# Two ConvFFNs, by both halves of the positions at once or by one half after the other, with the converted weights kept in DRAM

## The chip, the cores and the metric

The kernel runs on one core of one Trainium2 chip. The metric is the time of the program on the device in microseconds; the time of a kernel is the median of its runs. Beside the plain runs there is one execution under the hardware profiler, from which the page and the trace come. All numbers of single instructions are from that execution.

## What is computed

Two layers of a decoder trunk over 1024 positions of 1024 channels (batch 1, float32). Layer 0 is a hybrid mixer (attention and a state-space model), layer 1 a Conformer convolution module. Each is followed by a ConvFFN, and the change is about these two:

```python
def conv_ffn(h, up_w, conv_w, conv_b, down_w):
    u = causal_dwconv(h @ up_w.astype(h.dtype), conv_w, conv_b)     # width 3
    gate, val = u[..., :FFN_DIM], u[..., FFN_DIM:]                  # FFN_DIM = 2816
    return (jax.nn.silu(gate) * val) @ down_w.astype(h.dtype)

def conformer_conv(h, pw1_w, pw1_b, dw_w, dw_b, ln_w, ln_b, pw2_w, pw2_b):
    u = h @ pw1_w.astype(h.dtype) + pw1_b.astype(h.dtype)
    u = u[..., :CONF_WIDTH] * jax.nn.sigmoid(u[..., CONF_WIDTH:])
    u = causal_dwconv(u, dw_w, dw_b)                                # width 31
    u = jax.nn.silu(layer_norm(u, ln_w, ln_b))
    return u @ pw2_w.astype(h.dtype) + pw2_b.astype(h.dtype)

for i in range(DEPTH):
    ...
    x = x + conv_ffn(rms_norm(x, ffn_norm_w[i]), ffn_up_w[i], ffn_conv_w[i], ffn_conv_b[i], ffn_down_w[i])
```

## The kernel before, in words

The activations lie with channels on the 128 partitions and positions along the row: eight tiles of 1024 positions, handled as two halves of 512 (h = 0 and 1). The mixer takes the first part of the span and is not touched. What follows is `trunk_tail`: the FFN of layer 0, the Conformer, the FFN of layer 1.

**A product in two 16-bit parts.** `gemm` (line 234) multiplies float32 values as pairs of 16-bit parts: three matmuls (high x high, high x low, low x high) for each of the 8 tiles of the contraction, so 24 matmuls of 128x128 by 512 positions for one tile of one half. The weights' parts are made on the chip by `loads` (line 86): SP's queue loads a raw float32 tile (512 KB) into one of three `raw` buffers; ScalarE scales it into the high part (line 94 or 98); the low part comes either from VectorE in one step (line 99, `pool=False`) or from a second ScalarE step that scales raw in place (line 95) and a subtraction on GpSimd (line 96, `pool=True`). Both parts lie in one of four `w` buffers. The scale is a power of two found from the sum of squares of the whole matrix. These sums come from `scan` (line 138), which loads every weight once more through ScalarE's queue (line 150, two buffers in the trunk) and squares it there (line 147); `rooted`, `powers` and `conf_powers` turn the sums into scales, with small matmuls on TensorE (`total`, line 110) in between.

**The FFN by pairs and groups.** An FFN has 22 pairs (a gate tile and a value tile of 128 columns). `pair` (line 966) multiplies both up tiles, evicts them through the width-3 convolution (`conv3`, lines 946 to 954: one ScalarE step and two VectorE multiply-adds out of PSUM), applies SiLU (line 982) and the product (line 962, on GpSimd where the group is `pool=True`) and squares the result for a scale (line 963). A `Group` is some pairs for one or both halves. `close` turns a group's results into 16-bit parts (lines 936, 937) and `down` multiplies them by the group's rows of the down projection, eight output tiles, adding each to x (line 1065).

**How the work was cut.** Six pairs (BOTH) are done for both halves with one conversion of each weight; the other 16 pairs, as two groups of 8 (HALVES), for half 0 and later again for half 1, with a conversion each time. In layer 0 the order is: the six pairs for both halves, then the groups of half 0, then those of half 1 laid beside the Conformer of half 0. In layer 1: the groups of half 0 laid beside the Conformer of half 1, then the six pairs for both halves, then the groups of half 1. `first_pairs` (line 989) is the start of a both-halves group: two pairs whose four weight tiles are held, first for half 0, while the norm of half 1 (`rms`, line 910) is made after the first two tiles, then for half 1.

**The Conformer** goes half by half too: `p1` (line 1106) has 16 tiles of matmuls and, for each of eight channel tiles, 30 multiply-adds of 512 positions on VectorE (line 1125); `ln` (line 1137) is the LayerNorm, whose sums over the channels go through small matmuls (`token_sums`, line 904, and `bcast`, line 259); `p2` multiplies by the second weights. All Conformer weights are converted with `pool=True`, once for each half.

**What sets the order.** The functions are generators that yield an estimate of TensorE's time (5.2 for an up tile). `along(a, na, b, nb)` takes from b in the ratio nb/na while a goes on, `weave` puts a fixed gap of one generator between the steps of others, `beside` takes one step of the scans per yield, and `ahead` runs a generator for a given cost. What comes out is an order of priorities; loads are raised by AHEAD = 60 instructions and evictions by EV = 100, and a scheduler lays out each engine's instructions at build time. On the chip every engine and every queue then works in that order.

Of the kernel before, what the change touches and what calls it, by code (L numbers as in the profile page):

```python
# [14 lines left out]
F16 = mybir.dt.float16  # L15
# [13 lines left out]
BOTH = 6  # L29
HALVES = (8, 8)  # L30
# [15 lines left out]
class Net:  # L46
    def __init__(self, ctx, tc, I, out):
        self.tc, self.nc, self.I, self.out = tc, tc.nc, I, out
        self.sb = ctx.enter_context(tc.tile_pool(name="sb", bufs=1))
        self.n = 0  # L50
        self.pows, self.sums = {}, {}
# [34 lines left out]
    def loads(self, src, nk, scale, pool=False):  # L86

        nc = self.nc
        with self.tc.high_priority(offset=AHEAD):
# [7 lines left out]
            else:  # L97
# [4 lines left out]
                                               ALU.mult, ALU.subtract)  # L102
        return w
# [862 lines left out]
    def pair(self, G, i):  # L966
# [4 lines left out]
        for e, j2 in enumerate((G.k0 + i, NP + G.k0 + i)):  # L971
            w = self.loads(self.I["ffn_up_w"][G.l, j2], KT, self.pows[f"up{G.l}"][0], pool=G.pool)
            prev = None
            for h in G.hs:
# [12 lines left out]
                yield 5.2  # L987

    def first_pairs(self, G):

        r1 = self.rms(1, self.fnw[:, G.l, :])
        self.open(G)
        js = (G.k0, NP + G.k0, G.k0 + 1, NP + G.k0 + 1)
        G.have = 2
        ws = [self.loads(self.I["ffn_up_w"][G.l, k], KT, self.pows[f"up{G.l}"][0]) for k in js]
        keep = self.T("hf", [P, 2, 22, 2])
        for h in range(2):
            for i, j2 in enumerate(js):
                ps = self.PT("mm")
                self.gemm(ps[:], ws[i], self.hn[h])  # L1000
                with self.tc.high_priority(offset=EV):
                    a = self.conv3(G.l, j2, ps, keep[:, 0, i] if h else None)
                    if j2 < NP:
                        self.nc.scalar.activation(a[:], a[:], AF.Silu)
                        g = a
                    else:
                        self.gate(G, i // 2, h, g, a)
                    if h == 0:
                        self.nc.vector.tensor_copy(keep[:, 0, i], ps[:, HALF - 2:HALF])
                if h == 0 and i < 2:  # L1010
                    steps(r1, 1)
                yield 5.2
# [44 lines left out]
    def down(self, G, post=None):  # L1057
        for c in range(KT):
            w = self.loads(self.I["ffn_down_w"][G.l, c, :, G.k0:G.k0 + G.n, :], G.n,
                           self.pows[f"down{G.l}"][0], pool=G.pool)  # L1060
# [22 lines left out]
    def p1_tile(self, j, h):  # L1083
# [3 lines left out]
        wb = self.loads(self.I["conf_pw1_w"][KT + j], KT, sc, pool=True)  # L1087
# [5 lines left out]
        wa = self.loads(self.I["conf_pw1_w"][j], KT, sc, pool=True)  # L1093
# [74 lines left out]
    def p2(self, h):  # L1168
# [4 lines left out]
        for c in range(KT):  # L1173
            w = self.loads(self.I["conf_pw2_w"][c], KT, self.pows["pw2"][0], pool=True)
# [14 lines left out]
    def halves(self, l, k0):  # L1189

        nb, nh = HALVES
        halo = self.T("hf", [P, 2, 22, 2])
        hb, hc = halo[:, :, 0:nb], halo[:, :, nb:nb + nh]
        return ([Group(l, k0, nb, (h,), hb, pool=h != l) for h in range(2)],
                [Group(l, k0 + nb, nh, (h,), hc, pool=h != l) for h in range(2)])

    def trunk_tail(self):

        self.V, self.s = {}, {}
        A = Group(0, 0, BOTH, (0, 1))  # L1200
        B, C = self.halves(0, BOTH)
# [11 lines left out]
        f = chain(f, self.beside(chain(self.ups(C[1], (B[1], None)), self.call(self.powers, 1),  # L1213
# [191 lines left out]
```

## Time and profile before

| What | us |
|---|---|
| runs, median of 3 | 2300.31 (2294.36 to 2307.05) |
| the profiled execution | 2295.18 |
| its span, first to last instruction | 2293.4 |
| PE busy in the span | 2209.9 |
| mean granted TensorE clock | 0.982 |

The first 600 us or so are the mixer. The first matmul of layer 0's FFN starts at 604 us, the last of layer 1's ends just before 2289.5 us. In a row of a group, the number after x is the count, then come the busy time, the mean duration in ns, and after the bar the idle time of the engine just before these instructions, with what ended it. In a row of a stretch each engine has its busy time and its count, then come the clock that was granted to TensorE, the mean busy share of the 16 DMA engines, and GB/s.

### The profile page before, as it was taken

Reading aid. Unit: us, or ns where it says so; the run is one execution under the profiler, and the core shown is the slowest. Engines: PE = TensorE matmul, PEld = TensorE weight load, DVE = VectorE, ACT = ScalarE, POOL = GpSimd, SP = SyncE. Lnnn points to the kernel's source line nnn. Section 1 sums busy time; section 2 is a strip of 40 time slices with the busy share of each in tenths; the row PEclk is TensorE's granted clock in tenths of the full one; section 3 lists DMA queues with packets and bytes.
Section 4 is the critical chain, followed back from the end, with each engine's and each line's share of the span. In section 5 each row is a group of like instructions: output and inputs, shape, how many; then the busy total and the mean of one; then the engine's idle time right before and its main releaser. Section 6 shows DMA issues by size and latency. Waiting matters only on the chain. (4 is left out here: it accounts for less than half of the span.)

```text
span 2293.4 us, 28980 instructions
## 1 busy us (share of the span) xinstructions
PE 2209.9 (96%) x10767; PEld 1228.2 (54%) x10767; DVE 1549.3 (68%) x2923; ACT 1376.2 (60%) x2191; POOL 452.2 (20%) x336
## 2 busy tenths in 40 slices
PE   7999999889899999999999998999999999999999
PEld 7788987767544444444444444444444444444444
DVE  6976677776755547454789997699997164635763
ACT  7776556653566667576677756677877443514541
POOL 0000000123000000023545543445553400000000
PEclk9999999999899999999999999999999999999999
DMA  6434211221356576755223332333332321133332
GB/s 204 138 98 147 83 28 31 85 71 56 109 185 195 185 245 198 266 172 183 91 82 105 104 97 70 96 92 101 101 102 73 111 65 55 49 113 97 101 102 82
DMA packets 87885, 262.08 MB, mean 114 GB/s; under 512 B 12864, under 2 KB 15552, under 8 KB 87744
## 3 DMA queue, kind: packets, MB, share of 16 engines
q1 hardware_dynamic: 58368, 178.44, 25.1%
q10 hardware_dynamic: 29376, 81.80, 11.2%
q8 instruction: 84, 1.38, 0.2%
q14 instruction: 57, 0.47, 0.1%
HBM read 256.01 MB, written 4.19 MB: 113 GB/s over the span
## 5 line engine op out<-in xcount | busy, mean ns | idle before, releaser
L239 PEld LDWEIGHTS <-w 128*128 128x128 f16 x7488 | 737.2, 99 | 899.8 <-issue 31.1
L239 PE MATMUL pmm<-h,w 128*128 128x512 f16 x5376 | 1173.9, 381 | 10.9 <-DVE h L934 5.0
L239 PE MATMUL pmm<-g,w 128*128 128x512 f16 x2112 | 468.9, 384 | 0.0
L96 POOL TENSOR_TENSOR w<-raw,w 128x1024 f16<-128x1024 f32 x144 | 308.5, 2144 | 492.4 <-ACT raw L95 309.1
L952 DVE SCALAR_TENSOR_TENSOR a<-pmm,c_ffn_conv_w,a 128x511 f32<-128x511 f32 (+1 forms) x352 | 262.0, 746 | 174.3 <-ACT a L946 171.2
L1125 DVE SCALAR_TENSOR_TENSOR pt<-u,c_conf_dw_w,pt 128x512 f32<-128x512 f32 x480 | 339.7, 750 | 8.9 <-ACT pt L1122 5.4
L239 PE MATMUL pmm<-h,whl 128*128 128x512 f32 x912 | 231.8, 404 | 0.0
L147 ACT ACTIVATE scan<-scan 128x1024 f32<-128x1024 f32 (+2 forms) x204 | 173.1, 850 | 71.1 <-DMA scan<-ffn_up_w 45.0
L1065 DVE SCALAR_TENSOR_TENSOR x<-pmm,gs,x 128x512 f32<-128x512 f32 x96 | 71.9, 749 | 174.1 <-PE pmm L239 174.0
L239 PEld LDWEIGHTS pmm<-h,whl 128*128 128x128 f32 x912 | 167.7, 190 | 36.3 <-POOL whl L220 0.2
L429 PE MATMUL pmm<-whl,h 128*128 128x384 f32 (+1 forms) x672 | 137.7, 354 | 18.2 <-ACT h L230 11.5
L963 ACT ACTIVATE a<-g 128x512 f32<-128x512 f32 x88 | 55.3, 628 | 164.3 <-DVE g L962 83.7
L946 ACT ACTIVATE a<-pmm,c_ffn_conv_b,c_ffn_conv_w 128x512 f32<-128x512 f32 x112 | 86.4, 771 | 76.4 <-PE pmm L239 74.3
L429 PEld LDWEIGHTS pmm<-whl,h 128*128 128x128 f32 x672 | 119.3, 193 | 22.5 <-ACT h L230 11.8
L98 ACT ACTIVATE w<-raw,c_su_up 128x1024 f16<-128x1024 f32 x88 | 100.0, 1138 | 48.9 <-PE pmm L239 31.8
L99 DVE SCALAR_TENSOR_TENSOR w<-raw,c_su_up,w 128x1024 f16<-128x1024 f32 x88 | 112.6, 1280 | 18.2 <-ACT w L98 16.8
L98 ACT ACTIVATE w<-raw,c_su_down 128x1024 f16<-128x1024 f32 (+1 forms) x48 | 51.2, 1071 | 70.8 <-PE pmm L239 66.9
L982 ACT ACTIVATE a<-a 128x512 f32<-128x512 f32 x80 | 50.1, 627 | 52.9 <-DVE a L952 42.3
L94 ACT ACTIVATE w<-raw,c_su_pw 128x1024 f16<-128x1024 f32 x48 | 54.7, 1140 | 37.2 <-PE pmm L239 33.6
L94 ACT ACTIVATE w<-raw,c_su_up 128x1024 f16<-128x1024 f32 x64 | 72.6, 1138 | 6.8 <-PE pmm L239 6.8
L95 ACT ACTIVATE raw<-raw,c_su_up 128x1024 f32<-128x1024 f32 x64 | 73.2, 1146 | 2.1
L1032 POOL TENSOR_TENSOR hf<-hf,c_ffn_conv_w 128x8 f32<-128x8 f32 x8 | 4.5, 559 | 341.9 <-DVE hf L980 283.6
(316 smaller groups left out, 2333.6 us busy)
## 6 DMA issues: line engine op xcount, KB each, us to landing
raw<-ffn_up_w SPq DMA_DIRECT2D x152, 512.0 KB, 3.6
raw<-ffn_down_w SPq DMA_DIRECT2D x64, 512.0 KB, 3.5
raw<-conf_pw_w SPq DMA_DIRECT2D x48, 512.0 KB, 3.6
scan<-ffn_up_w ACTq DMA_DIRECT2D x88, 256.0 KB, 3.1
scan<-ffn_up_w ACTq DMA_DIRECT2D x44, 512.0 KB, 4.6
scan<-ffn_down_w ACTq DMA_DIRECT2D x32, 512.0 KB, 4.1
scan<-conf_pw_w ACTq DMA_DIRECT2D x24, 512.0 KB, 4.3
raw<-w_out SPq DMA_DIRECT2D x16, 448.0 KB, 3.3
```

The source lines that it names most:

```text
L94: nc.scalar.activation(w[:, 0], raw[:], AF.Copy, scale=scale)
L95: nc.scalar.activation(raw[:], raw[:], AF.Copy, scale=scale)
L96: nc.gpsimd.tensor_sub(w[:, 1], raw[:], w[:, 0])
L98: nc.scalar.activation(w[:, 0], raw[:], AF.Copy, scale=scale)
L99: nc.vector.scalar_tensor_tensor(w[:, 1].rearrange("p k m -> p (k m)"), raw.rearrange("p k m -> p (k m)"), scale, w[:, 0].rearrange("p k m ...
L147: nc.scalar.activation(t, t, AF.Square, accum_out=sums[:, k:k + 1])
L239: self.nc.tensor.matmul(ps, w[:, a, k, :], h[:, b, :], start=n == 0, stop=n == last)
L429: nc.tensor.matmul(ps[:, 0:n], h[:, a, tc_], ws[k // 2][:, b, k % 2, :], start=i == 0, stop=i == 3 * KT - 1)
L946: nc.scalar.activation(a[:], ps[:], AF.Identity, bias=b, scale=w[:, 2:3])
L952: nc.vector.scalar_tensor_tensor(a[:, d:], ps[:, 0:HALF - d], wd, a[:, d:], ALU.mult, ALU.add)
L1065: self.nc.vector.scalar_tensor_tensor(self.xs(c, h), ps[:], G.u[h], self.xs(c, h), ALU.mult, ALU.add)
L1125: nc.vector.scalar_tensor_tensor(y[:], u[:, k:k + HALF], w[:, k:k + 1], y[:], ALU.mult, ALU.add)
```

## The change

Every group now covers one half: 8, 8 and 6 pairs for half 0, then the same for half 1, in both layers. The weights are loaded in float32 and converted in the first half only. The 16-bit parts are then written from the `w` buffer to a DRAM tile, by a DMA on GpSimd's queue, and in the second half loaded from there straight into a `w` buffer, by SP, with no conversion. The Conformer's weights get the same treatment. `first_pairs` is gone, and the norm of half 1 is woven elsewhere: in layer 0 after eight tiles of the first group (in which two steps of the scans are taken per yield), in layer 1 into the last part of half 0's FFN, behind the Conformer's second product. The numbers that lay FFN work beside the Conformer change from 190 and 215 to 285 and 270.

```diff
-BOTH = 6
-HALVES = (8, 8)
+GROUPS = 8, 8, 6
...
-    def loads(self, src, nk, scale, pool=False):
+    def loads(self, src, nk, scale, pool=False, key=None):
         nc = self.nc
+        if key in self.made:
+            with self.tc.high_priority(offset=AHEAD):
+                w = self.T("w", [P, 2, nk, P], F16)
+                nc.sync.dma_start(w[:], self.made.pop(key)[:])
+            return w
...
+        if key is not None:
+            name = "made_" + "_".join(str(k) for k in key)
+            self.made[key] = self.dram.tile([P, 2, nk, P], F16, name=name, tag=name, bufs=1)
+            nc.gpsimd.dma_start(self.made[key][:], w[:])
         return w
...
-            w = self.loads(self.I["ffn_up_w"][G.l, j2], KT, self.pows[f"up{G.l}"][0], pool=G.pool)
+            w = self.loads(self.I["ffn_up_w"][G.l, j2], KT, self.pows[f"up{G.l}"][0], G.pool,
+                           None if len(G.hs) == 2 else ("up", G.l, j2))
...
-        wb = self.loads(self.I["conf_pw1_w"][KT + j], KT, sc, pool=True)
+        wb = self.loads(self.I["conf_pw1_w"][KT + j], KT, sc, True, ("pw1", KT + j))
...
+    def groups(self, l):
         halo = self.T("hf", [P, 2, 22, 2])
+        res = [[], []]
+        for h in range(2):
+            k = 0
+            for n in GROUPS:
+                res[h].append(Group(l, k, n, (h,), halo[:, :, k:k + n], pool=h != l))
+                k += n
+        return res
...
-        f = self.first_pairs(A)
-        for _ in f:
-            steps(bg, 1)
-        f = chain(self.ups(A), self.ups(B[0], (A,), "down0"), self.ups(C[0], (B[0],)))
-        f = chain(f, self.ups(B[1], (C[0], self.stat_add), ahead=2))
-        f = self.beside(f, bg)
-        ahead(f, 4 * 20.8 + 8 * 10.4 + 8 * 7.8 + 8 * 10.4 + 8 * 5.2 + 2 * 10.4 + 5.2)
+        f = self.beside(self.ups(A[0]), bg, 2)
+        ahead(f, 4 * 10.4)
+        self.weave(f, 10, self.rms(1, self.fnw[:, 0, :]))
+        run(f)
+        run(self.beside(chain(self.ups(A[1], (A[0],), "down0"), self.ups(A[2], (A[1],))), bg))
+        f = self.beside(self.ups(B[0], (A[2], self.stat_add), ahead=2), bg)
+        ahead(f, 2 * 10.4 + 3.9)
         self.conf_powers()
-        ahead(f, 8 * 5.2)
+        ahead(f, 8 * 3.9)
         self.weave(f, 10, self.rms(0, self.cnw))
...
-        along(chain(self.p1(0), self.ln(0)), 212, f, 190)
+        along(chain(self.p1(0), self.ln(0)), 212, f, 285)
...
-        along(chain(p1, self.ln(1)), 206, f, 215)
+        along(chain(p1, self.ln(1)), 206, f, 270)
+        ahead(f, 15)
+        run(self.p2(1))
+        self.weave(f, 10, self.rms(1, self.fnw[:, 1, :]))
         run(f)
-        run(self.p2(1))
-        run(self.first_pairs(E))
-        run(self.ups(E))
-        run(self.ups(B[1], (E, lambda c, h: h or self.store(c, h))))
-        run(self.ups(C[1], (B[1], None)))
-        f = self.down(B[1])
-        ahead(f, 2 * 5.2)
-        self.close(C[1])
-        run(f)
-        run(self.down(C[1], self.store))
+        run(self.ups(B[0]))
+        run(self.ups(B[1], (B[0],)))
+        run(self.ups(B[2], (B[1], None)))
+        run(self.finish(B[1], B[2], self.store))
```

After the change A is a layer's three groups of half 0 and B those of half 1.

More of the change, by code (lines that the diff above doesn't have):

```diff
@@ L50, in __init__ @@
         self.n = 0
-        self.pows, self.sums = {}, {}
+        self.pows, self.sums, self.made = {}, {}, {}
+        self.dram = ctx.enter_context(tc.tile_pool(name="dram", bufs=1, space=bass.MemoryType.DRAM))
     @contextmanager
@@ L986, in pair @@
                 prev = ps[:, HALF - 2:HALF]
[L987 to L1011, printed above, removed]
                 yield 5.2
@@ L1059, in down @@
             w = self.loads(self.I["ffn_down_w"][G.l, c, :, G.k0:G.k0 + G.n, :], G.n,
-                           self.pows[f"down{G.l}"][0], pool=G.pool)
+                           self.pows[f"down{G.l}"][0], G.pool,
+                           None if len(G.hs) == 2 else ("down", G.l, G.k0, c))
             for h in G.hs:
@@ L1092, in p1_tile @@
                              scale=self.u1[:, 0:1])
-        wa = self.loads(self.I["conf_pw1_w"][j], KT, sc, pool=True)
+        wa = self.loads(self.I["conf_pw1_w"][j], KT, sc, True, ("pw1", j))
         pa = self.PT("mm")
@@ L1173, in p2 @@
         for c in range(KT):
-            w = self.loads(self.I["conf_pw2_w"][c], KT, self.pows["pw2"][0], pool=True)
+            w = self.loads(self.I["conf_pw2_w"][c], KT, self.pows["pw2"][0], True, ("pw2", c))
             ps = self.PT("mm")
@@ L1187, in weave @@
                 ahead(f, gap)
[L1189 to L1191 removed]
+    def groups(self, l):
         halo = self.T("hf", [P, 2, 22, 2])
[L1193 to L1195 removed]
+        res = [[], []]
[5 more added lines that the diff above has]
+        return res
     def trunk_tail(self):
         self.V, self.s = {}, {}
[L1200 to L1201 removed]
+        A, B = self.groups(0)
         bg = chain(self.scan_down(0), self.scan_conf(), self.scan_up(1), self.scan_down(1))
[L1203 to L1209 removed]
+        f = self.beside(self.ups(A[0]), bg, 2)
[5 more added lines that the diff above has]
+        ahead(f, 2 * 10.4 + 3.9)
         self.conf_powers()
[L1211 removed]
+        ahead(f, 8 * 3.9)
         self.weave(f, 10, self.rms(0, self.cnw))
[L1213 to L1214 removed]
+        f = chain(f, self.beside(chain(self.ups(B[1], (B[0],)), self.ups(B[2], (B[1], None)),
+                                       self.call(self.powers, 1),
+                                       self.finish(B[1], B[2], self.stat_add)), bg))
         self.hal = self.T("eh", [P, KT, 30])
[L1216 removed]
+        along(chain(self.p1(0), self.ln(0)), 212, f, 285)
         run(f)
@@ L1225, in trunk_tail @@
         self.weave(p1, 3, self.rms(0, self.fnw[:, 1, :]))
-        B, C = self.halves(1, BOTH)
-        E = Group(1, 0, BOTH, (0, 1))
-        f = chain(self.ups(B[0]), self.ups(C[0], (B[0], None), "down1"), self.finish(B[0], C[0]))
-        along(chain(p1, self.ln(1)), 206, f, 215)
-        run(f)
-        run(self.p2(1))
-        run(self.first_pairs(E))
-        run(self.ups(E))
-        run(self.ups(B[1], (E, lambda c, h: h or self.store(c, h))))
-        run(self.ups(C[1], (B[1], None)))
-        f = self.down(B[1])
-        ahead(f, 2 * 5.2)
-        self.close(C[1])
-        run(f)
-        run(self.down(C[1], self.store))
+        A, B = self.groups(1)
+        f = chain(self.ups(A[0]), self.ups(A[1], (A[0],), "down1"), self.ups(A[2], (A[1], None)),
+                  self.finish(A[1], A[2], self.store))
+        along(chain(p1, self.ln(1)), 206, f, 270)
+        ahead(f, 15)
+        run(self.p2(1))
+        self.weave(f, 10, self.rms(1, self.fnw[:, 1, :]))
+        run(f)
+        run(self.ups(B[0]))
+        run(self.ups(B[1], (B[0],)))
+        run(self.ups(B[2], (B[1], None)))
+        run(self.finish(B[1], B[2], self.store))
     def call(self, f, *a):
@@ L1245, in call, with beside @@
         yield
-    def beside(self, f, bg):
+    def beside(self, f, bg, n=1):
         for d in f:
-            next(bg, None)
+            steps(bg, n)
             yield d
```

1 line of the change is left out of this document (removed).

## The prediction

> **What bounds the kernel now.** I read the page first, then the busy time by stretches, then the stretches where TensorE loses time, and last the waits in them. In the page, TensorE is busy almost throughout, and nearly all of it is one helper's matmuls:
>
> ```profile
> span 2293.4 us, 28980 instructions
> PE 2209.9 (96%) x10767; PEld 1228.2 (54%) x10767; DVE 1549.3 (68%) x2923; ACT 1376.2 (60%) x2191; POOL 452.2 (20%) x336
> ...
> L239 PE MATMUL pmm<-h,w 128*128 128x512 f16 x5376 | 1173.9, 381 | 10.9 <-DVE h L934 5.0
> L239 PE MATMUL pmm<-g,w 128*128 128x512 f16 x2112 | 468.9, 384 | 0.0
> L96 POOL TENSOR_TENSOR w<-raw,w 128x1024 f16<-128x1024 f32 x144 | 308.5, 2144 | 492.4 <-ACT raw L95 309.1
> ```
>
> The 7488 matmuls of the two FFNs and the Conformer keep an even beat where nothing disturbs them; the chain that ended last has this piece, 124.32 / 576 = 0.2158 us each, 5.18 us per tile of 24:
>
> ```profile
> 1863.95 124.32 PE pmm L239 x576
> ```
>
> By stretches (columns: stretch, its length, then busy time and count of PE, PEld, DVE, ACT, POOL, the granted clock, DMA share, GB/s):
>
> ```profile
> 840.00:885.00 45.00, 45.00 (x211) 20.39 (x209) 28.20 (x42) 33.15 (x55) 4.07 (x9) 1.00 0.69 232
> 915.00:965.00 50.00, 50.00 (x234) 22.65 (x232) 20.29 (x23) 29.06 (x44) 0.00 (x0) 1.00 0.78 261
> 1120.00:1290.00 170.00, 169.79 (x789) 76.94 (x787) 149.51 (x241) 122.34 (x146) 83.97 (x55) 1.00 0.31 96
> 1630.00:1720.00 90.00, 90.00 (x420) 40.95 (x418) 84.61 (x137) 67.41 (x81) 49.65 (x30) 1.00 0.33 100
> 1860.00:2260.00 400.00, 400.00 (x1864) 182.44 (x1862) 233.76 (x370) 165.28 (x237) 3.58 (x12) 1.00 0.27 84
> ```
>
> In all five TensorE is full. So the conversions of weights that the change drops from the last 400 us (VectorE at 0.58, ScalarE at 0.41) are hidden today and buy nothing there. What differs is the margin: beside the Conformer VectorE is at 0.88 to 0.94; in layer 0's first FFN the DMA share is 0.69 to 0.78.
>
> TensorE's losses lie at the seams of the Conformer. These are the same matmuls (L239 alone: PE, PEld, clock, DMA) in the six stretches where time is lost:
>
> ```profile
> 1105.00:1120.00 15.00, 11.23 (x40) 4.37 (x39) 0.77 0.23 71
> 1290.00:1310.00 20.00, 16.21 (x63) 6.78 (x61) 0.83 0.36 105
> 1370.00:1430.00 60.00, 46.51 (x190) 19.66 (x188) 0.91 0.21 62
> 1470.00:1490.00 20.00, 15.79 (x68) 6.79 (x66) 0.91 0.26 79
> 1620.00:1630.00 10.00, 7.35 (x35) 3.44 (x35) 1.00 0.28 102
> 1720.00:1750.00 30.00, 22.03 (x85) 9.14 (x84) 0.89 0.24 70
> ```
>
> At 0.2158 us these 481 matmuls are 103.8 of the 155 us. The small matmuls on PSUM tile pt, which the change keeps, are busy there for the sum of this row:
>
> ```profile
> sum 155.00, PE 13.85; mean PE 2.31
> ```
>
> So 155 - 103.8 - 13.9 = 37 us are lost: about 6.4, 5.5, 11.8, 4.3, 2.1 and 7.3 by stretch. That is the most this change can win at the seams. Four rows of TensorE's waits name who was late, always VectorE or what feeds it:
>
> ```profile
> PE pmm L239 <- DVE h L934: 5.0, 3, 3.3
> PE pt L904 <- DVE rb L1152: 4.9, 2, 2.9
> PE pt L904 <- ACT h L1129: 4.0, 2, 2.6
> PE pt L110 <- DVE tiny L132: 3.7, 2, 3.3
> ```
>
> Waits explain a part; the clock the rest: it is below 1.00 in five of the six. A second mechanism sits in these seams. The timeline shows one VectorE add taking three times as long while a weight conversion runs on GpSimd (L96, here 2.38 us):
>
> ```profile
> 1734.86 2.38 POOL L96 TENSOR_TENSOR w<-raw,w 128x1024 f16<-128x1024 f32 x1 [8.43 <-ACT raw L95]
> ...
> 1735.77 2.03 DVE L1152 TENSOR_TENSOR rb<-rb,a 128x512 f32<-128x512 f32 x1
> ```
>
> The min, median and max of that add's 14 show how rare the long form is:
>
> ```profile
> L1152 DVE TENSOR_TENSOR rb<-rb,a x14: 674/684/2076, 1380.7 to 1741.9; 128x512 f32<-128x512 f32 x14
> ```
>
> **The change part by part.**
>
> *TensorE's work* keeps its count: each up tile meets each half once, and so does each down tile of a group, however the groups are cut. Halving every group moves no matmul out or in. Price 0.
>
> *Conversions.* GpSimd's 144 become 44 + 24 (layer 1, first half) + 16 + 8 (Conformer, first half) = 92. VectorE's lose the 68 of layer 1's second half, hidden as shown. What counts is where the 52 of GpSimd go from: layer 0's second half loses all 48 and the Conformer's second half 24, while layer 1's first half gains 20. So the seams at 1105, 1290 and 1370 lose most of their 2 us collisions, those at 1470 some, and those at 1620 and 1720 none.
>
> *More work beside the Conformer's convolution.* Its fillers were cut to 190 and 215 us for a convolution costed at 212 and 206; now 285 and 270. By the costs in the code, the first one has 193 of its own, so the FFN work laid beside it goes from 193 x 190/212 = 173 to 193 x 285/212 = 259 us. With the Conformer's own 16 tiles (16 x 5.18 = 83) the stage is 256, then 342 us. VectorE's load there by the row of 1120:1290 is 0.88 x 256 = 225 us. The added 86 us bring about 0.3 x 86 = 26 us (two multiply-adds per up tile and one per down tile; all have the form of the row below, 0.75 us). So (225 + 26) / 342 = 0.73 in place of 0.88, and layer 1 comes down alike. Nothing is removed from VectorE here; it is spread, so its queue should be short when a sum that TensorE waits for joins it.
>
> ```profile
> L1065 DVE SCALAR_TENSOR_TENSOR x<-pmm,gs,x 128x512 f32<-128x512 f32 x96 | 71.9, 749 | 174.1 <-PE pmm L239 174.0
> ```
>
> Together: by seam I take 6.4 to 2, 5.5 to 2.5, 11.8 to 4, 4.3 to 3, 2.1 to 1, 7.3 to 4, in all 37 to 16.5: a gain of 21. Bounds: 37 if every seam closes, and 0 if each is only the length of its own chain (square, add, eight times over, then reciprocal root), which no load shortens.
>
> *The norm of the second half* leaves the first two tiles and comes after eight. Its 16 small matmuls filled a hole at the start, where TensorE waits for the first weights anyway:
>
> ```profile
> 601.16 3.15 PE L904 MATMUL pt<-c_ones,rb 128*128 128x1 f32 x14 [0.53 <-DVE rb L817]
> ...
> 607.66 11.49 PE L239 MATMUL pmm<-h,w 128*128 128x512 f16 x44 [1.63 <-DVE w L99]
> ```
>
> The hole stays and the 16 come later: loss 0 to 16 x 3.15/14 = 3.6, I take 2. In layer 1 the same norm is put before the rest of the first half's FFN, by the code's costs 343 - 241 (beside the convolution) - 15 - 20 = 67 us, in place of the two tiles; the row of 1860:2260 shows no loss from it before, price 0.
>
> *Stores.* 44 + 24 stores per layer and 24 of the Conformer go out through GpSimd's queue. No row shows a DMA issued there. Bounds per issue: the 0.33 us of a scan's on ACT's queue to the 2.14 of L96.
>
> ```profile
> 844.43 0.33 ACTq L150 DMA_DIRECT2D scan<-ffn_up_w  x1
> ...
> L962 POOL TENSOR_TENSOR g<-a,a 128x512 f32<-128x512 f32 x32 | 41.9, 1309 | 40.9 <-DVE a L952 27.4 <-DVE hf L980 8.1 <-DVE c_su_down L125 4.5
> ```
>
> GpSimd's fullest stretch becomes layer 1's first half: per tile a conversion 2.13, half a gate 0.65, an issue 0.3 to 2.1, 3.1 to 4.9 of 5.18 us. Behind a store stand the next conversion and gate; four w buffers (15 us ahead) cover that. The loads back have the size and queue of those they replace (512 KB on SP), three tiles ahead. Price 0; if the cover goes, GpSimd at 4.9 plus the running sums of the Conformer would be over the beat.
>
> *Bandwidth in layer 0's first half* is the dear item. The first half now handles every tile for one half only, so each 5.18 us brings a 512 KB load, as in 840:885, and a 512 KB store, 101 GB/s more. The scans of the next weights keep running there, at two per tile asked for in the first group. 232 + 101 = 333 GB/s, and by the row's own ratio share 0.69 x 333/232 = 0.99; by 915:965 it is 0.78 x 362/261 = 1.08. The phase is 44 x 5.18 + 8 x (5.18 + 5.18 + 3.89) = 342 us. If the DMA engines were the bound, it would grow by up to 8%, 27 us. If the scans merely end later, in the second half, where loads are the only other traffic, it costs 0. I take 5, near the row at 0.99. The Trainium skill speaks against this part: DMA: Bandwidth & Descriptors, Rules for kernel authors, says that spreading transfers over queues gives no bandwidth, as all run on the same 16 engines. Its Specifications put the fabric's ceiling at 435 GB/s, by which 333 would be a share of 0.77 and the cost 0; the trace's own ratio puts the ceiling at 335, and I go by the trace.
>
> The shorter last group (6 pairs) changes only how the last downs are cut; the last eviction stays. Price 0.
>
> Sum: the profiled execution took 2295.2 us (2293.4 span); 2295.2 - 21 + 2 + 5 = 2281. The median of the three runs lies 5.1 above the profiled one, so 2286.
>
> **Rivals.**
>
> *The DMA engines set the pace of layer 0's first half* (slower). The scans run on ScalarE in order between evictions and conversions, through two buffers. In the same 45 us:
>
> ```profile
> L147 ACT ACTIVATE scan<-scan 128x1024 f32<-128x1024 f32 x12 | 12.6, 1046 | 1.6 <-DMA scan<-ffn_up_w 1.6
> ...
> L946 ACT ACTIVATE a<-pmm,c_ffn_conv_b,c_ffn_conv_w 128x512 f32<-128x512 f32 x9 | 6.9, 772 | 5.1 <-PE pmm L239 4.9
> ...
> L147 ACT ACTIVATION_READ_ACCUMULATOR scan<-scan 128x1 f32 x11 | 2.1, 188 | 0.0
> ```
>
> and the scans' median time to landing:
>
> ```profile
> scan<-ffn_up_w ACTq DMA_DIRECT2D x44, 512.0 KB, 4.6
> ```
>
> One buffer comes round every 2 x 45/12 = 7.5 us and needs 4.6 + 1.05 + 0.19 + 0.33 = 6.2: landings may grow by 1.3 us. Beyond that ScalarE stops at the square, and conversion and eviction behind it stop too; its 4.9 us of waiting for TensorE are the last cover. At a landing of 7.2 us twelve scans take 6 x 8.8 - 4.9 = 48 us for 45, 6% of 342, as much as the seams give: from there the change loses. At 7.7 it is 6 x 9.3 - 4.9 = 50.7, 12.7%, 43 us: 2300 - 21 + 2 + 43 = 2324. For it: share 0.99. Against: at 0.78 TensorE was still full, and the demand falls as the pace does. Chance 0.20.
>
> *The seams are chain lengths* (no change): the 21 shrink to 5 or so, 2300 - 5 + 2 + 3 = 2300. For it: at 1720 the collisions with L96 stay, and TensorE's waits there are for the last link of a chain. Against: VectorE was fully booked in each. Chance 0.27.
>
> *Stores and VectorE hold each other up*: if an issue on GpSimd holds VectorE as L96 does, 2.03 - 0.68 = 1.4 us per tile, and a quarter of the 68 reach TensorE, 24 us: 2300 - 21 + 2 + 24 = 2305. Against: VectorE idles 16.8 of 45 us there. The Trainium skill has the reverse lock, in SBUF — State Buffer, under "SBUF: two separate sides": GpSimd cannot write a DMA's descriptors while VectorE runs in a two-port mode. No run here shows a store from GpSimd yet; the collision of L96 with L1152 agrees with a lock between these two engines. Chance 0.05.
>
> **How the numbers follow.** 0.5% of 2300.3, what a measurement of this kernel can tell from no change, is 11.5 us: faster below 2288.8, slower above 2311.8. Forecast 0.48 (2286), its own range 2265 to 2295. Range: from all seams closed and nothing paid, 2300 - 37 = 2263, to the bandwidth rival at 2324. Faster 0.48, same 0.27 + 0.05, slower 0.20.
>
> **What would show it.** Right: L96 x92; the six seams at 16 us lost or less; VectorE near 0.75 beside the convolution; the adds L1152 and L896 at 0.7 us in the first Conformer's norm; layer 0's first half at 342 us with DMA share 0.95. Wrong: idle time of TensorE before L239 in layer 0's first half behind w or L147, scan landings over 7 us, or a seam that keeps its wait with VectorE idle before it.

## The result and the profile after

| Kernel | runs, median (us) | ratio to before, 95% interval | profiled span (us) |
|---|---|---|---|
| before | 2301.64 (2294.36 to 2307.05) | | 2293.4 |
| changed | 2327.7 (2325.92 to 2329.2) | 1.0115 (1.0096 to 1.0134) | 2326.0 |

The changed kernel is 1.15% slower. (The median before has one run more than the table ahead of the prediction.) The forecast was 2286, and the measured time lies 4 us beyond the upper end of the range, 2324. Here are the lines of the changed kernel's page that answer to those shown of before (the FFN's helper is now L249, GpSimd's conversion L102, the scan's square L157):

```profile
span 2326.0 us, 29102 instructions
...
PE 2217.2 (95%) x10767; PEld 1231.7 (53%) x10767; DVE 1472.7 (63%) x2835; ACT 1193.2 (51%) x2019; POOL 449.4 (19%) x480
...
PE 71%; DMA 10%; DVE 10%; ACT 5%; issue 2%; POOL 1%; ACTq 0%; SPq 0%; DVEq 0%; POOLq 0%
...
L249 PE MATMUL pmm<-h,w 128*128 128x512 f16 x5376 | 1188.0, 383 | 31.7 <-ACT w L104 16.3
L249 PE MATMUL pmm<-g,w 128*128 128x512 f16 x2112 | 461.0, 380 | 0.0
L102 POOL TENSOR_TENSOR w<-raw,w 128x1024 f16<-128x1024 f32 (+1 forms) x92 | 192.7, 2094 | 309.0 <-ACT raw L101 308.7
L157 ACT ACTIVATE scan<-scan 128x1024 f32<-128x1024 f32 (+2 forms) x204 | 173.6, 852 | 139.8 <-DMA scan<-ffn_up_w 67.4
```

VectorE and ScalarE have 77 and 183 us less to do, GpSimd's conversions fell from 144 to 92 as foreseen, and still the span grew by 32.6 us. Two lines say where to look: TensorE now waits 31.7 us before the up products, over half of it for ScalarE's conversion L104, and ScalarE idled 139.8 us before the squares of the scans (71.1 before), mostly for their DMAs. The chain that ended last holds 10% DMA.

The same stretches as in the prediction (the columns are busy time and count of PE, PEld, DVE, ACT, POOL, then clock, DMA share, GB/s):

```profile
840.00:885.00 45.00, 40.59 (x179) 18.00 (x177) 32.96 (x56) 32.49 (x52) 9.17 (x20) 0.92 0.79 273
915.00:965.00 50.00, 46.65 (x214) 20.37 (x213) 17.09 (x23) 25.95 (x41) 3.20 (x6) 1.00 0.89 301
1120.00:1290.00 170.00, 170.00 (x791) 77.23 (x790) 133.69 (x209) 63.45 (x84) 40.75 (x45) 1.00 0.41 133
1860.00:2260.00 400.00, 398.61 (x1859) 181.89 (x1858) 156.96 (x276) 125.17 (x188) 53.69 (x61) 1.00 0.38 123
```

Of the first two, full before, TensorE loses 4.4 and 3.4 us, with ScalarE at 0.72 and 0.52: nothing is saturated, something is late. The last two are full as before.

To see the whole, I took three long stretches of the gemm helper's matmuls alone: roughly layer 0's FFN in its first half (604 to 1100), the first Conformer (1100 to 1700) and the second Conformer (1700 to 1900). First the changed kernel, then the kernel before:

```profile
604.00:1100.00 496.00, 448.43 (x1986) 197.13 (x1986) 0.94 0.81 280
1100.00:1700.00 600.00, 589.79 (x2717) 266.11 (x2716) 1.00 0.44 142
1700.00:1900.00 200.00, 187.72 (x848) 83.78 (x847) 0.97 0.51 160
```

```profile
604.00:1100.00 496.00, 490.94 (x2253) 221.12 (x2254) 0.99 0.62 200
1100.00:1700.00 600.00, 571.23 (x2580) 255.29 (x2579) 0.98 0.31 94
1700.00:1900.00 200.00, 189.26 (x857) 84.72 (x856) 0.98 0.29 85
```

A stretch's length less its count x 0.2158 us is what TensorE lost there (the small matmuls are counted as loss, in both kernels alike). Before: 9.8, 43.2, 15.1. Changed: 67.4, 13.7, 17.0. So TensorE loses 57.6 us more in the first stretch, 29.5 less in the second and 1.9 more in the third. Together +30.0, for a span that grew by 32.6: the account closes but for 2.6. (The profiled execution before lies 6 us under its median, so the medians differ by 26.)

The bounds are fixed times, and one seam crosses 1100: the first small matmul of the norm in front of the first Conformer starts at 1083.42 in the kernel before and at 1034.97 in the changed one. Cut there, TensorE loses 8.1 us before and 58.1 in the changed kernel up to this norm (2184 matmuls in 479.42 us, 1728 in 430.97), and 44.9 and 23.2 from it to 1700 (2649 in 616.58, 2974 in 665.03). So the change paid 50.0 us in layer 0's first half, won 21.7 at the first Conformer's seams, and won nothing at the second's. The 50.0 is the entry to explain.

In that stretch (604 to 1110), these are ScalarE's waits, total, times and longest; first the changed kernel, then before:

```profile
ACT scan L157 <- DMA scan<-ffn_up_w: 54.6, 26, 4.8
ACT scan L157 <- DMA scan<-ffn_down_w: 36.1, 25, 4.2
ACT scan L157 <- DMA scan<-conf_pw_w: 33.1, 15, 3.8
ACT a L956 <- PE pmm L249: 14.1, 13, 3.0
```

```profile
ACT a L946 <- PE pmm L239: 36.0, 31, 2.2
ACT scan L147 <- DMA scan<-ffn_up_w: 33.0, 17, 3.5
...
ACT scan L147 <- DMA scan<-conf_pw_w: 11.9, 7, 4.0
ACT scan L147 <- DMA scan<-ffn_down_w: 10.2, 9, 4.3
```

The waits for scans went from 55.1 to 123.8 us, and ScalarE's wait for TensorE at this eviction, a measure of its slack, from 36.0 to 14.1. The landings of the scans grew less than the rival asked for (4.6 us before); the stores land slowly, but no wait of ScalarE or TensorE there ends with one (SP's queue waits for a store once, 7.3 us):

```profile
made_up<-w POOLq DMA_DIRECT2D x88, 512.0 KB, 5.5
...
scan<-ffn_up_w ACTq DMA_DIRECT2D x44, 512.0 KB, 5.8
...
made_down<-w POOLq DMA_DIRECT2D x32, 512.0 KB, 6.4
```

What TensorE waited for between 604 and 1100 in the changed kernel:

```profile
PE pmm L249 <- ACT w L104: 16.3, 3, 11.3
PE pt L120 <- DVE tiny L1031: 13.9, 2, 9.5
PE pmm L249 <- DVE w L105: 5.7, 6, 1.6
```

All three come from ScalarE. How a late scan gets there is seen in the timeline of the second one, the sum that `close` needs:

```profile
954.84 0.63 ACT L993 ACTIVATE a<-a 128x512 f32<-128x512 f32 x1 [1.66 <-DVE hf L991]
959.51 1.06 ACT L157 ACTIVATE scan<-scan 128x1024 f32<-128x1024 f32 x1 [4.05 <-DMA scan<-ffn_up_w]
...
960.57 0.76 ACT L956 ACTIVATE a<-pmm,c_ffn_conv_b,c_ffn_conv_w 128x512 f32<-128x512 f32 x1
...
961.36 1.53 DVE L962 SCALAR_TENSOR_TENSOR a<-pmm,c_ffn_conv_w,a 128x511 f32<-128x511 f32 x2 [6.55 <-ACT a L956]
...
975.04 0.16 DVE L1031 TENSOR_REDUCE tiny<-gm 128x1 f32<-128x6 f32 x1 [2.92 <-ACT a L973]
975.25 0.59 PE L120 MATMUL pt<-tiny,c_ones 128*128 128x1 f32 x2 [9.52 <-DVE tiny L1031]
```

A square sits in ScalarE's order ahead of the eviction L956. Its data comes 4.05 us late, the eviction starts late, VectorE idles 6.55 us behind it, and after five more scan squares between the evictions, four of which wait too, the square of the group's last product (L973), its sum and with it TensorE are 9.5 us late. The other large stall, 11.33 us up to 688, has the same form at the norm of half 1: its casts L943 alternate with squares, three of which wait (4.21, 1.81 and 0.92 us, the first before TensorE stops), and the conversion L104 stands behind them.

### The profile page after: what moved, and what is told of

The parts are those of the page before. It is cut to its first block, busy times and chain, and to the rows that moved or that the text cites. A ratio compares the mean times of both kernels' runs of the same rounds, so it can differ in the third digit from the quotient of the medians.

```text
span 2326.0 us, 29102 instructions
## 1 busy us (share of the span) xinstructions
PE 2217.2 (95%) x10767; PEld 1231.7 (53%) x10767; DVE 1472.7 (63%) x2835; ACT 1193.2 (51%) x2019; POOL 449.4 (19%) x480
## 3 DMA queue, kind: packets, MB, share of 16 engines
q1 hardware_dynamic: 64128, 197.31, 28.5%
q10 hardware_dynamic: 29376, 81.80, 10.3%
## 4 chain that ended last, share of the span: by engine, by line
PE 71%; DMA 10%; DVE 10%; ACT 5%; issue 2%; POOL 1%; ACTq 0%; SPq 0%; DVEq 0%; POOLq 0%
PE pmm L249 59%; DMA scan<-ffn_up_w 5%; PE pmm L439 4%; DMA scan<-conf_pw_w 2%; DMA scan<-ffn_down_w 2%; DVE a L962 2%; DVE pt L1112 1%; ACT scan L157 1%; PE pt L559 1%; PE pt L439 1%; DVE h L944 1%; PE pt L718 1%; PE pt L544 1%; DVE g L947 1%; PE pt L727 1%
## 5 line engine op out<-in xcount | busy, mean ns | idle before, releaser
L249 PEld LDWEIGHTS <-w 128*128 128x128 f16 x7488 | 737.2, 99 | 927.0 <-issue 32.3
L249 PE MATMUL pmm<-h,w 128*128 128x512 f16 x5376 | 1188.0, 383 | 31.7 <-ACT w L104 16.3
L249 PE MATMUL pmm<-g,w 128*128 128x512 f16 x2112 | 461.0, 380 | 0.0
L962 DVE SCALAR_TENSOR_TENSOR a<-pmm,c_ffn_conv_w,a 128x511 f32<-128x511 f32 x352 | 262.7, 747 | 121.0 <-ACT a L956 115.5
L102 POOL TENSOR_TENSOR w<-raw,w 128x1024 f16<-128x1024 f32 (+1 forms) x92 | 192.7, 2094 | 309.0 <-ACT raw L101 308.7
L157 ACT ACTIVATE scan<-scan 128x1024 f32<-128x1024 f32 (+2 forms) x204 | 173.6, 852 | 139.8 <-DMA scan<-ffn_up_w 67.4
L249 PE MATMUL pmm<-h,whl 128*128 128x512 f32 x912 | 231.4, 404 | 0.0
L249 PEld LDWEIGHTS pmm<-h,whl 128*128 128x128 f32 x912 | 167.7, 190 | 36.2 <-POOL whl L230 0.2
L958 ACT ACTIVATE a<-pmm,c_ffn_conv_b,c_ffn_conv_w 128x510 f32<-128x510 f32 x88 | 67.8, 772 | 161.7 <-PE pmm L249 161.3
L973 ACT ACTIVATE a<-g 128x512 f32<-128x512 f32 x88 | 55.2, 627 | 174.3 <-POOL g L972 111.9
L959 DVE SCALAR_TENSOR_TENSOR a<-pmm,c_ffn_conv_w,hf 128x2 f32<-128x2 f32 x88 | 19.2, 218 | 145.3 <-ACT a L958 145.1
L112 POOL DMA_DIRECT2D made_up<-w x88 | 49.5, 562 | 245.8 <-DVE w L105 228.0
L972 POOL TENSOR_TENSOR g<-a,a 128x512 f32<-128x512 f32 x44 | 57.7, 1311 | 179.5 <-DVE a L962 123.2
L993 ACT ACTIVATE a<-a 128x512 f32<-128x512 f32 x88 | 55.1, 626 | 71.6 <-DVE a L962 55.4
L956 ACT ACTIVATE a<-pmm,c_ffn_conv_b,c_ffn_conv_w 128x512 f32<-128x512 f32 x88 | 67.5, 768 | 40.4 <-PE pmm L249 38.2
L105 DVE SCALAR_TENSOR_TENSOR w<-raw,c_su_up,w 128x1024 f16<-128x1024 f32 x44 | 56.2, 1280 | 45.0 <-ACT w L104 45.0
L947 DVE SCALAR_TENSOR_TENSOR g<-g,gs,g 128x512 f16<-128x512 f32 x88 | 64.5, 776 | 7.2 <-ACT g L946 7.1
L946 ACT ACTIVATE g<-g,gs 128x512 f16<-128x512 f32 x88 | 57.0, 709 | 13.1 <-DVE gs L136 12.8
```

What stands on the lines that cost most here:

```text
L102: nc.gpsimd.tensor_sub(w[:, 1], raw[:], w[:, 0])
L157: nc.scalar.activation(t, t, AF.Square, accum_out=sums[:, k:k + 1])
L249: self.nc.tensor.matmul(ps, w[:, a, k, :], h[:, b, :], start=n == 0, stop=n == last)
L946: nc.scalar.activation(dst[:, 0], src, AF.Copy, scale=s)
L947: nc.vector.scalar_tensor_tensor(dst[:, 1], src, s, dst[:, 0], ALU.mult, ALU.subtract)
L956: nc.scalar.activation(a[:], ps[:], AF.Identity, bias=b, scale=w[:, 2:3])
```

## The experiments

The theory after the result: the stores slow the landing of the scans; ScalarE, which works in order and has only two scan buffers, stops at the squares; conversions and evictions behind them come late. Its rivals: the 16 DMA engines are simply full, the scans are too dense at the start, or the halving itself (a conversion for each tile, the norm's new place) costs the time. The seams are a question of their own. All kernels differ from the changed one except `e4_before_plus_stores` and `e11_before_three_buffers`, which differ from the kernel before. The columns give the measured time, its ratio to the kernel before as run in the same round (medians of 2300.99 to 2303.09), and what TensorE lost in the three stretches with fixed bounds, worked out as above. "Up to the norm" below means the cut at the norm in front of the first Conformer.

| Kernel | median us | ratio to before (95%) | 604-1100 | 1100-1700 | 1700-1900 |
|---|---|---|---|---|---|
| before | 2301.64 | | 9.8 | 43.2 | 15.1 |
| changed | 2327.7 | 1.0115 (1.0096 to 1.0134) | 67.4 | 13.7 | 17.0 |
| e1_no_store0 | 2304.16 | 1.0011 (1.0001 to 1.0021) | 34.0 | 20.6 | 19.6 |
| e2_scans_late | 2329.94 | 1.0137 (1.0114 to 1.016) | 69.8 | 13.0 | 17.0 |
| e3_three_scan_buffers | 2290.45 | 0.9957 (0.9942 to 0.9972) | 29.7 | 13.2 | 19.4 |
| e4_before_plus_stores | 2315.1 | 1.0064 (1.0048 to 1.008) | 30.7 | 43.7 | 15.3 |
| e5_three_buffers_norm_later | 2282.98 | 0.9919 (0.9904 to 0.9934) | 22.1 | 13.7 | 19.4 |
| e6_along_as_before | 2328.85 | 1.011 (1.0092 to 1.0128) | 72.2 | 18.4 | 11.4 |
| e7_norm_later | 2322.04 | 1.008 (1.006 to 1.0099) | 64.2 | 13.7 | 17.0 |
| e8_four_scan_buffers | 2288.61 | 0.994 (0.9925 to 0.9955) | 27.7 | 13.7 | 19.4 |
| e9_gpsimd_busy_again | 2344.96 | 1.0177 (1.0149 to 1.0205) | 76.9 | 23.6 | 13.8 |
| e10_four_buffers_norm_later | 2280.55 | 0.9904 (0.9885 to 0.9924) | 17.4 | 15.6 | 18.7 |
| e11_before_three_buffers | 2300.51 | 0.9993 (0.9979 to 1.0007) | 9.8 | 43.5 | 20.9 |

**Layer 0 without stores** (its second half converts again):

```diff
-                           None if len(G.hs) == 2 else ("up", G.l, j2))
+                           None if G.l == 0 else ("up", G.l, j2))
...
-                           None if len(G.hs) == 2 else ("down", G.l, G.k0, c))
+                           None if G.l == 0 else ("down", G.l, G.k0, c))
```

> The changed kernel without the 68 stores of layer 0's FFN; its second half loads float32 and converts again. Between 604 and 1100 us the changed kernel loses 66 us of TensorE (the kernel before 8). Theory A, memory traffic: the stores bring the DMA share to 0.8 to 0.97, the scans' landings grow from 4.6 to 5.8 us, and ScalarE stands at the scans' squares with conversions and evictions queued behind. Without them landings fall to 4.6 to 5.0, the loss to 20 or less, and the whole to about 2328 - 46 + 8 (conversions back in the second half) = 2290. Theory B, ScalarE's order: the denser order of scans between the conversions is the cost, whatever the traffic: the loss stays at 50 to 65 and the time at 2320 to 2335.

Half of the loss goes (67.4 to 34.0): the scans land in 4.5 us again, and ScalarE waits 42 us for them instead of 124. Up to the norm it is 58.1 to 26.2, against 8.1 before: 32 of the 50.0 us go with the stores, and 18 stay, so the stores are not all of it. What stays comes with the rest of the change, the halving and the norm's new place, and this run does not take it apart. The seams lose 7 us more than in the changed kernel between 1100 and 1700.

**The last scans moved behind the first half:**

```diff
-        bg = chain(self.scan_down(0), self.scan_conf(), self.scan_up(1), self.scan_down(1))
+        bg = chain(self.scan_down(0), self.scan_conf())
...
+        run(bg)
+        bg = chain(self.scan_up(1), self.scan_down(1))
         f = self.beside(self.ups(B[0], (A[2], self.stat_add), ahead=2), bg)
```

> The changed kernel with the scans of layer 1's weights (up and down, 68 of the 116) begun only with layer 0's second half, where the weights come from DRAM and the DMA share is 0.4. Theory A: the first half has stores but from the second group on fewer scans; the loss after 800 us goes (about 35 of the 66), that of the first group (21 between 604 and 700) stays: 2328 - 35 = 2293. Theory B says the same of the later part, since the scans leave the order too; this run is for where scans cost nothing. If the scans are not the cause but the stores alone (w buffers held until a store lands), nothing changes: 2328.

It decides nothing: the squares did not move. From 604 to 700 and in the four hundreds after it there are 46, 44, 40, 50 and 45 of them, against 44, 44, 42, 48 and 48 in the changed kernel. The place in the source is a priority only, and the scheduler put the scans as early as before. What sets their pace is not shown: with three and with four buffers 48, 48 and 46 squares fall in the first three of these, four more than with two, and the fourth buffer adds none. In the kernel before, 48 fall in the first, so the changed kernel's start isn't denser in scans either.

**A third scan buffer** (paid for with two buffers of g):

```diff
-TRUNK = {"raw": 3, "w": 4, "g": 20, "sv": 1, "hf": 3, "scan": 2, "gm": 4, "gs": 4, "sums": 5}
+TRUNK = {"raw": 3, "w": 4, "g": 18, "sv": 1, "hf": 3, "scan": 3, "gm": 4, "gs": 4, "sums": 5}
...
-    def scan_up(self, l, depth=2):
+    def scan_up(self, l, depth=3):
...
```

The same goes for the other two scans, and the size of a piece, which the code ties to the depth, stays at 512 KB.

> The changed kernel with three scan buffers in place of two, three loads in flight (two buffers of g less to make room). If the landing time is what ScalarE waits for (latency), a buffer has half as much time again before its square and the waits mostly go: loss 66 to 25, 2328 - 40 = 2288. If it is the 16 engines' throughput, three in flight only land later (8 us) and the loss stays: 2320 to 2330. Theory B (order alone) also says no change.

This is the run that tells the theory from the full DMA engines. Every store stays, TensorE loses 29.7 in place of 67.4, and the kernel beats the one before by 0.43%. ScalarE's waits in 604 to 1110 in this kernel:

```profile
ACT scan L156 <- DMA scan<-conf_pw_w: 18.3, 12, 3.5
ACT scan L156 <- DMA scan<-ffn_up_w: 15.3, 11, 2.7
ACT scan L156 <- DMA scan<-ffn_down_w: 13.2, 8, 4.0
```

They are 47 us, below those of before, though one landing now takes longer (6.8 us for scan<-ffn_up_w, with three of them under way). The row of 800 to 900 for the gemm helper, in this kernel and in the changed one:

```profile
800.00:900.00 100.00, 100.00 (x465) 45.30 (x463) 1.00 0.92 334
```

```profile
800.00:900.00 100.00, 95.15 (x432) 42.76 (x431) 0.97 0.86 296
```

TensorE is full at 334 GB/s and a share of 0.92. The changed kernel lost 6.8 of these 100 us at 296 GB/s: the engines could carry more than it asked for.

**The stores alone, in the kernel before** (layer 0's two groups of half 0, 32 up and 16 down tiles, written, and read by nobody):

```diff
...
+        if key is not None:
+            name = "made_" + "_".join(str(k) for k in key)
+            made = self.dram.tile([P, 2, nk, P], F16, name=name, tag=name, bufs=1)
+            nc.gpsimd.dma_start(made[:], w[:])
         return w
...
```

> The kernel before, with the 16-bit parts of layer 0's half-0 groups (32 up tiles, 16 down tiles) also stored to DRAM from GpSimd's queue; nothing reads them. Theory A: from about 745 us on the traffic is that of the changed kernel, landings grow to 5.8, and TensorE loses 20 to 35 us that it did not lose: 2301 + 25 = 2326. Theory B: the order of ScalarE is that of the kernel before, so nothing is lost: 2300 to 2304.

48 stores cost 13 us in the median and 21 in the first stretch, and nothing elsewhere; the scans land in 5.4 us and ScalarE waits 101 us for them. So the stores do harm by themselves, in the old order of work too.

**A third buffer in the kernel before:** the edit of `e3_three_scan_buffers`, and one step of the scans ahead of the first pairs.

> The kernel before with three scan buffers (g at 18, one scan step more at the start). Control: there landings of 4.6 us fit two buffers and TensorE loses nothing between 700 and 1000, so a third buys nothing: 2298 to 2304. If three buffers help by themselves, whatever the stores, it falls by more than 8 us.

No change: 0.9993, and 9.8 lost in the first stretch as before. ScalarE waits 18 us for its scans instead of 55, and TensorE gains nothing, which fits the slack that ScalarE had there. In the changed kernel the buffer buys about as much as leaving out the stores (25.9 and 26.2 us lost up to the norm), so it seems to repair what the stores broke; a third buffer in the changed kernel without stores was not run.

**A fourth scan buffer** (scan 4, g 16):

> Four scan buffers (g at 16). If the landing time against the ring is the cause, what three buffers left after 800 us (6 us) goes too and the time is 2283 to 2290; the casts' part between 604 and 800 stays at 20. If the engines' throughput becomes the bound with four loads in flight, the DMA share goes to 1.0 and the time back up, over 2295.

ScalarE's waits for scans fall to 6 us and TensorE's loss only from 29.7 to 27.7. From three buffers on, the scans are no longer what is late.

**The norm of half 1 later,** in the third group (after the second group's eight pairs, eight down tiles and one more pair) instead of after eight tiles of the first; two, three and four scan buffers:

```diff
-        ahead(f, 4 * 10.4)
+        run(f)
+        f = self.beside(chain(self.ups(A[1], (A[0],), "down0"), self.ups(A[2], (A[1],))), bg)
+        ahead(f, 8 * 10.4 + 8 * 5.2 + 10.4)
         self.weave(f, 10, self.rms(1, self.fnw[:, 0, :]))
         run(f)
-        run(self.beside(chain(self.ups(A[1], (A[0],), "down0"), self.ups(A[2], (A[1],))), bg))
```

> The changed kernel (two scan buffers) with the norm of half 1 moved into the third group. Theory C: the stall of 11.3 us at 676 goes with its half-speed clock; the loss between 604 and 800 falls from 28 to 15, that after 800 grows a little where the casts now stand: 2328 - 10 = 2318. Theory D: 2325 to 2332.

> Three scan buffers as in the run before, and in layer 0 the norm of half 1 moved from the ninth tile of the first group into the third group. With three buffers 22 of the remaining 28 us are lost between 604 and 800, around the norm's eight casts on ScalarE, which stand between scans and conversions. Theory C, the norm's place: a first group with a conversion per tile and a scan or two has no room on ScalarE for eight casts; moved, the loss there falls to about 10 and the time to 2290 - 12 = 2278. Theory D: the start has no weights in advance and the scans alone fill ScalarE there; the loss stays at 20 and the time at 2288 to 2292.

> Four scan buffers and the norm of half 1 in the third group. Three buffers with the norm moved took 2283; four against three alone were worth 2 us, inside the runs' spread. So 2279 to 2285: the landing is already covered by three, and what is left lies at the second Conformer's seam.

Moving the norm is worth 3.2, 7.6 and 10.3 us of the first stretch with two, three and four buffers (3.2, 7.7 and 8.1 up to the norm in front of the Conformer). With four buffers that is over half of what this part still loses above the kernel before, 21.8 against 8.1. With both, the kernel takes 2280.55 us, 0.96% less than before and 2.0% less than the changed kernel (2280.55 / 2327.7, from different rounds). The first stretch of this best version:

```profile
604.00:1100.00 496.00, 484.72 (x2218) 217.23 (x2217) 0.99 0.82 291
```

17.4 us lost, 7.6 more than before, at a DMA share of 0.82, a hair above the changed kernel's 0.81.

**The ratio beside the convolution as before** (285 to 190, 270 to 215):

```diff
-        along(chain(self.p1(0), self.ln(0)), 212, f, 285)
+        along(chain(self.p1(0), self.ln(0)), 212, f, 190)
...
-        along(chain(p1, self.ln(1)), 206, f, 270)
+        along(chain(p1, self.ln(1)), 206, f, 215)
```

> The changed kernel with the two ratios that lay FFN work beside the Conformer set back to 190 and 215. The prediction put the gain at the Conformer's seams to VectorE's work being spread. If so, the seams of the first Conformer (1100 to 1500 us: 40 us lost before, 8 in the changed kernel) lose 25 or more again and the time goes to about 2345. If the gain is from GpSimd's conversions being gone, which hold up VectorE's adds, the loss stays at about 8 and the time at 2328.

VectorE's load beside the first convolution (1120 to 1360) goes up; the changed kernel first, then this one:

```profile
1120.00:1360.00 240.00, 240.00 (x1116) 109.16 (x1115) 192.90 (x311) 93.68 (x129) 54.13 (x57) 1.00 0.40 128
```

```profile
1120.00:1360.00 240.00, 237.96 (x1123) 110.16 (x1122) 214.36 (x363) 102.75 (x147) 54.48 (x64) 1.00 0.39 125
```

0.89 in place of 0.80, the old load, and yet the first Conformer loses 18.4 and not 43 (25.9 from the norm on, against 23.2 and 44.9); the second even less than in the changed kernel. The time is the same. So the new ratio is not needed for the seams to stay closed. GpSimd's conversions are away in this kernel, and the new ratio is in place in `e1_no_store0` and `e9_gpsimd_busy_again`, where GpSimd has work again; no run with this cut of the work has both as before, so it is not ruled out that either alone would do.

**GpSimd busy again in layer 0's second half,** with a subtraction nobody reads, the size of the conversion that was dropped:

```diff
                 nc.sync.dma_start(w[:], self.made.pop(key)[:])
+                if key[0] in ("up", "down") and key[1] == 0:
+                    nc.gpsimd.tensor_sub(self.T("raw", [P, nk, P])[:], w[:, 0], w[:, 1])
             return w
```

> The changed kernel with a subtraction of the old size on GpSimd (128x1024, about 2.1 us, into a raw buffer that nothing reads) after each of the 68 loads from DRAM in layer 0's second half, without ScalarE's two conversion steps: it puts GpSimd's share of the old work back, and only that. If the collisions of GpSimd's conversions with VectorE's adds made the seams, the first Conformer (1100 to 1500 us) loses 20 us or more again in place of 8, and the time goes to 2340. If ScalarE's steps did, the loss stays near 8 and the time at 2328.

The seams lose 9.9 us more between 1100 and 1700 (13.7 to 23.6). The adds of the norms between 1000 and 1550, before, in the changed kernel and in this one (count, busy time, mean ns):

```profile
L896 DVE TENSOR_TENSOR rb<-rb,a 128x512 f32<-128x512 f32 x21 | 19.2, 917 | 9.6 <-ACT a L895 9.5
```

```profile
L906 DVE TENSOR_TENSOR rb<-rb,a 128x512 f32<-128x512 f32 x20 | 13.8, 691 | 19.9 <-ACT a L905 19.8
```

```profile
L908 DVE TENSOR_TENSOR rb<-rb,a 128x512 f32<-128x512 f32 x21 | 18.8, 897 | 16.6 <-ACT a L907 16.6
```

917, 691 and 897 ns: with GpSimd at work the long form is back. But the long adds aren't where the 9.9 us are. They take 2.63, 2.57 and 1.03 us, start at 1024.19, 1028.19 and 1034.27, each beside a subtraction, and belong to the norm in front of the Conformer, so to the first stretch. Between 1100 and 1700 TensorE's longest wait is 5.3 us up to 1383.94, for a small sum (0.65 us at the same place in the changed kernel). VectorE takes up the copy that leads to it 5.5 us after the matmuls before it, behind convolution steps of their usual 0.75 us. One add of 1.60 us, at 1415.84, is in that stretch. The order of the work differs there, and collisions are not shown as the cause of that wait. Of the 9.5 us more in the first stretch, 6.7 are lost before the first subtraction, at 957, and stay unexplained.

The seam in front of the Conformer is the one that the change did not close. VectorE's other step of the norm, the low part of its result, is there still long, before and in the changed kernel (minimum, median, maximum in ns, 1000 to 1550):

```profile
L934 DVE TENSOR_TENSOR h<-a,h x24: 676/680/2614, 1098.4 to 1490.0; 128x512 f16<-128x512 f32 x24
```

```profile
L944 DVE TENSOR_TENSOR h<-a,h x24: 675/679/4447, 1051.7 to 1521.5; 128x512 f16<-128x512 f32 x24
```

The 4.45 us are at 1053.06, while GpSimd works through a product (1.25 us) and the conversion of a Conformer weight (2.12 us), and TensorE waits 3.8 us there for these steps, as it did before. The Conformer's first half still converts, which the prediction left out when it took the collisions out of this seam.

## Why the prediction was wrong, point by point

**The failing step is "Bandwidth in layer 0's first half", of which it said "I take 5".** Up to the norm in front of the Conformer the changed kernel lost 50.0 us more than the kernel before. Some 32 of them go when the stores are left out, and 32 when the ring gets a third buffer. The step and its rival had the right suspects: the stores, the scans' two buffers, ScalarE's order. Two things in it were wrong.

- *The form of the limit.* It asked whether the 16 engines would be full (share 0.99 expected, 0.81 measured over 604 to 1100). They were not, and with more buffers they moved more (292 GB/s with three) at a smaller loss. What counted was the time of one landing in a ring of two. The step's ceiling of 335 GB/s was too low as well: 334 went at a share of 0.92, which makes 363. The 435 GB/s that the Trainium skill (DMA: Bandwidth & Descriptors, Specifications) gives as the fabric's ceiling, taken as the scale, would make the share of 334 0.77. The row has 0.92, and no run here went above 377 GB/s in any slice of its page.
- *The slack of the ring.* 7.5 us a round against 6.2 needed left 1.3 us, and the rival decided only from a landing of 7.2 us. The landing rose to 5.8, and the loss, 50.0, was larger than the rival's 43 us. The 7.5 is an average over 45 us in which the scans waited 1.6 us in all. In the whole stretch the kernel before waited 55 us for scans, so its ring was already short much of the time: the squares stand in ScalarE's order in ones and twos between other work, and a pair in a row (624.85 and 625.89) leaves a round far shorter than 7.5. ScalarE's slack, 36 us of waiting for TensorE at one eviction, hid that; a third buffer there gained nothing. The view that would have shown it is the waits of ScalarE over the whole half, and the step used them for a calm piece only.

**The rival on the slow side** named the right chain (a late scan stops ScalarE, conversions and evictions stop behind it) under the wrong heading, full engines. The added and removed stores and the rings of two, three and four show the chain. They do not show what the other 18 us of the 50.0 are; a part is the norm's new place.

**The norm's new place, priced at 2:** too low. With four scan buffers, where it stands almost alone, the later place is worth 8.1 us up to the Conformer's norm, and 8 in the time; with two it can't be told from the scans well (3.2).

**The seams, 37 to 16.5:** for the seams up to 1700 the forecast was a gain of 17.6, and 21.7 came out (44.9 to 23.2, the small matmuls counted as loss in both); for the last it was 3.3, and nothing came out (15.1 to 17.0). That the sum, near 20, lies close to the 21 is luck: the seam in front of the first Conformer, which was to go from 6.4 to 2, stayed (8.0 us lost in the 60 us from its norm on before, 9.1 changed), the one after 1700 stayed, and those between closed further than foreseen. At the second GpSimd still converts, and the first two of TensorE's waits between 1100 and 1900 in the changed kernel lie there, at 1816 and 1846. The third, at 1512, is in the first Conformer's last seam, and was 2.10 us long before the change too:

```profile
PE pt L914 <- DVE rb L1139: 3.0, 1, 3.0
PE pmm L249 <- POOL w L102: 2.9, 1, 2.9
PE pmm L249 <- ACT h L943: 2.1, 1, 2.1
```

The add that is the end of the first of these keeps its long form there (minimum, median, maximum in ns):

```profile
L1139 DVE TENSOR_TENSOR rb<-rb,a x14: 680/684/1569, 1383.7 to 1814.7; 128x512 f32<-128x512 f32 x14
```

Neither of the two reasons for the gain is shown to be its cause. GpSimd's collisions with VectorE's adds went with the conversions and came back with the subtractions. From the norm on, though, putting the conversions back whole costs 5.3 us of the 21.7 (28.5 lost), and GpSimd's part alone 13.4 (36.6), 5 of them in a wait without a long add. The spreading by the ratio is not needed: with the old ratio VectorE is as loaded as before and the seams stay closed (25.9). So at least 8 us of the gain are left unexplained. That half 1 now has three groups to lay over the seams in place of two is a candidate, and so is that either of the two reasons alone would do; neither was tried.

**Smaller steps.** VectorE beside the convolution came out at 0.79 (133.69 of 170), where 0.73 was worked out and 0.75 expected. The stores cost VectorE nothing: the conversion's low part takes 1.28 us in both kernels, and an issue on GpSimd 0.56 us, inside the bounds of 0.33 to 2.14. The lock of which the Trainium skill speaks in SBUF — State Buffer, "SBUF: two separate sides", was not seen on these stores. VectorE's steps with two inputs beside GpSimd's tensor work are what grew long, to 2.63 us in the run with GpSimd busy again and to 4.45 us in the changed kernel. The conversions dropped from the last 400 us bought nothing, as said: 1860 to 2260 was full and stayed so.

## What to carry to other kernels

Cost new DMA traffic by what it does to the landing time of the transfers that some engine waits for in order, and compare that with how deep their ring is; a DMA share well under 1 proves nothing. Read the slack of a ring from the waits of the engine over the whole stage, and not from an average round in a calm piece. When a change brings traffic, give the rings beside it one more buffer in the same step: here that turned 1.2% slower into 0.4% faster, and with the norm moved out of the crowded start into 0.8% faster (1.0% with a fourth buffer). And when a stage is compared before and after, cut it at an event of the program, not at a time: here a fixed bound moved a seam of 8 us from one stage to the next.

## What the runs showed of the hardware that was not expected

A landing stretches well before the engines are full: 512 KB on ScalarE's queue took 4.6 us at 200 GB/s and a share of 0.62, and 5.8 us at 280 GB/s and 0.81, with the same two under way. And a stall of TensorE costs more than its length. After the 11.33 us up to 688 the granted clock was down, as the rows of all engines show:

```profile
680.00:690.00 10.00, 1.03 (x2) 0.13 (x2) 7.48 (x14) 8.26 (x15) 0.00 (x0) 0.50 0.34 98
690.00:700.00 10.00, 9.81 (x32) 3.66 (x33) 4.81 (x5) 5.54 (x10) 1.60 (x3) 0.69 0.77 261
```

In the second of these TensorE is busy for 9.81 us and gets 32 matmuls done, at 0.2158 us each 6.9 us of work: another 3 us lost. That is 0.307 us for each, and 0.2158 / 0.307 = 0.70, near the granted 0.69.
